# An attention, gate and MLP block in split float32: two W_out blocks moved ahead of the projection, and the MLP's right factors laid out in two pools

## The chip, the cores and the metric

The kernel runs on one core of one Trainium2 chip. The metric is the device time of one execution in microseconds (us); lower is better. Inputs, weights and output are float32 in device memory, 1024 tokens of width 1024.

## The reference

```python
y = jax.nn.sigmoid(gate_a) * (o_a @ w_up_nsa[l]) + jax.nn.sigmoid(gate_b) * (o_b @ w_up_swa[l])
h = h + rms_norm(y @ w_out[l], norm_mix_post[l])
u = rms_norm(h, norm_mlp_pre[l])
f = jnp.square(jax.nn.relu(u @ w_mlp_in[l])) @ w_mlp_out[l]
h = h + rms_norm(f, norm_mlp_post[l])
```

`o_a` (sparse attention with compressed, selected and window keys) and `o_b` (window attention with sinks) are made by the first half of the kernel, which the change leaves as it is. `w_out` is 1024x1024, `w_mlp_in` 1024x4096, `w_mlp_out` 4096x1024.

## The kernel before

Every matrix is kept as two halves: a rounded high part (ACT copies it, `split` L81-91 or `load_w` L108) and the rest, a low part (a subtraction on DVE, L91, or shared between DVE with five eighths and POOL with three eighths, L116). A product is then three matmuls, high with high, high with low and low with high (`mm3`). So a weight block that comes from device memory passes a DMA into `wraw`, ACT (`wh`) and DVE, at times with POOL (`wl`), before TensorE (PE) can use both halves.

The stages that matter here, in order:

- **Gates** (L755-774). Eight rounds over `dc`, 128 columns of the two up-projections each. A round loads the up weights and two gate tiles `gt`, runs four groups of 12 matmuls, multiplies by the sigmoid (DVE L771, L773) and splits the result into `yh[c]`, `yl[c]`, for the two halves `c` of the tokens. The left inputs lie in `oh0`..`oh7`, `ol0`..`ol7`.
- **Output projection** (`out_proj` L822-839), four calls, two blocks of 128 tokens each. A call goes over eight blocks of W_out, 128x1024 (512 KB): load and split by `load_w`, then 12 matmuls L124-126. There are two `wraw` slots in pool `wq`; the first call puts `wh`, `wl` in `wq` too, the others in pool `we`. In the calls on `c` = 0 the low part is shared by DVE and POOL, in those on `c` = 1 DVE makes it alone.
- **Norms and transposes**, then **MLP1** (`prod` L957-959), seven products of a Strassen-like scheme over pairs of 128 columns; its right factors are `bh[i]`, `bl[i]` (and a seventh, `bh7h`, `bh7l`, in tiles tagged u7). Its results are combined (c, q; L1035-1066) and stored to device memory as seven operands `f_d`.
- **MLP2** (`product` L1145-1165), seven products in the order 1, 2, 5, 3, 6, 4, 7, each of 8 steps `kc` and 24 matmuls a step. A step needs `fh`, `fl` (from `fraw`, loaded by L1135 from `f_d`) and `vh`, `vl` (from a tile `b` of w_mlp_out, L1104). Each of the four names has four buffers in pool `st2`; `fraw` has three.

The code is written in the order above and a list scheduler decides the place of each instruction in its engine's queue; pools decide which memory lies over which. `st2` takes the memory that MLP1's right factors leave: `vh` over factor 3, `vl` over 6, `fh` over 4, `fl` over the u7 tiles. So the first writes into `fh` and `fl` have to follow MLP1's last readers of those factors. In `out_proj` the two `wraw` slots lie over `oh2`, `oh3`, which the last group of gate matmuls reads. SP issues most loads, in one queue; ACT issues the two loads of `x` (`hb`, L845); POOL the last five `fraw` and last three `b` of the first MLP2 product.

Of the kernel before, what the change touches and what calls it, by code (L numbers as in the profile page):

```python
# [8 lines left out]
F32 = mybir.dt.float32  # L9
F32R = mybir.dt.float32r  # L10
# [5 lines left out]
P = 128  # L16
# [12 lines left out]
CUT = (5, 5)  # L29
# [5 lines left out]
WEB = 3  # L35
# [10 lines left out]
NG = 4  # L46
# [6 lines left out]
def tile_hybrid_block(ctx: ExitStack, tc: tile.TileContext, x, norm_mix_pre, norm_mix_post, norm_mlp_pre,  # L53
                      norm_mlp_post, w_in, cmp_pos_k, cmp_w1_k, cmp_w2_k, cmp_pos_v, cmp_w1_v, cmp_w2_v,
                      attn_sinks, rel_bias, w_up_nsa, w_up_swa, w_out, w_mlp_in, w_mlp_out, onehot, out):
    nc = tc.nc
    x, out, w_in = x[0], out[0], w_in[0]
    w_up_nsa, w_up_swa, w_out, w_mlp_in, w_mlp_out = (w[0] for w in (w_up_nsa, w_up_swa, w_out, w_mlp_in, w_mlp_out))

    def pool(name, bufs=1, side="left", space=None):  # L60
        kw = {} if space is None else {"space": space}
        if space is not DRAM:
            kw["reuse_waits"] = "tile"
        if space is None:
            kw["side"] = side
        return tc.tile_pool(name=name, bufs=bufs, **kw)
# [17 lines left out]
    def split(h, l, src, h_eng="act", l_eng="dve"):  # L84

        if h_eng == "act":
            nc.scalar.activation(h, src, AF.Copy)  # L87
        else:
            nc.vector.tensor_copy(h, src)
        eng = nc.vector if l_eng == "dve" else nc.gpsimd  # L90
        eng.tensor_tensor(l, src, h.bitcast(F32), op=ALU.subtract)  # L91
# [80 lines left out]
    with ExitStack() as s_u:  # L172
# [8 lines left out]
        kc = pv.tile([P, 2, 2, HD], F32R, name="kc")  # L181
# [27 lines left out]
        with ExitStack() as s:  # L209
# [6 lines left out]
            vh = vt.tile([P, NB, NV], F32R, name="vh")  # L216
            vl = vt.tile([P, NB, NV], F32R, name="vl")
# [25 lines left out]
            with ExitStack() as s0:  # L243
# [28 lines left out]
                for b in range(NB):  # L272
# [11 lines left out]
                    r = rstd_of(tp, ss)  # L284
# [455 lines left out]
    with ExitStack() as s:  # L740
        s_y = s.enter_context(ExitStack())
        yp = [s_y.enter_context(pool("y0", side="right")), s_y.enter_context(pool("y1", side="right"))]
        yh = [p.tile([P, NB, 512], F32R, name="yh", tag="yh") for p in yp]
        yl = [p.tile([P, NB, 512], F32R, name="yl", tag="yl") for p in yp]
        s_ps = s.enter_context(ExitStack())
        pp = s_ps.enter_context(pool("ps2", space=PSUM))
        ps_any = lambda: pp.tile([P, 512], F32, name="ps", tag="ps", bufs=6)
        with s_ot:
            dp = s_ot.enter_context(pool("dtmp"))
            for dc in range(8):  # L750
                cs = slice(dc * P, (dc + 1) * P)
                wh, wl = load_w([((slice(None), slice(0, 4), slice(None)),
                                  w_up_nsa[:, cs].rearrange("(k p) c -> p k c", p=P)),
                                 ((slice(None), slice(4, 8), slice(None)),
                                  w_up_swa[:, cs].rearrange("(k p) c -> p k c", p=P))], [8, P])  # L755
                sig = []
                for b in range(2):
                    gt = dp.tile([P, T], F32, name="gt", tag="gt", bufs=4)
                    nc.sync.dma_start(gt, gate_d[b * D + dc * P:b * D + (dc + 1) * P, :])
                    nc.scalar.activation(gt, gt, AF.Sigmoid)  # L760
                    sig.append(gt)
                for c in range(2):
                    ts = slice(c * 512, (c + 1) * 512)
                    t = []
                    for b in (1, 0):
                        ps = ps_any()
                        for k in range(4):
                            kk = b * 4 + k
                            mm3(ps, wh[:, kk, :], wl[:, kk, :], oh_[kk][:, ts], ol_[kk][:, ts], k == 0, k == 3)
                        tt = dp.tile([P, 512], F32, name="tt", tag="tt", bufs=4)  # L770
                        nc.vector.tensor_tensor(tt, ps, sig[b][:, ts], op=ALU.mult)  # L771
                        t.append(tt)
                    nc.vector.tensor_tensor(t[0], t[0], t[1], op=ALU.add)  # L773
                    split(yh[c][:, dc, :], yl[c][:, dc, :], t[0])
        s_w.close()


# [8 lines left out]
        wp2 = s_w2.enter_context(pool("wq"))  # L786
# [14 lines left out]
        eh = s_e.enter_context(pool("etmph"))  # L801
        hb_e.update({b: eh.tile([P, D], F32, name="hb", tag="hb", bufs=2) for b in (0, 1)})
        s_we = s_e.enter_context(ExitStack())
        we = s_we.enter_context(pool("we"))
        wor = w_out.rearrange("(k p) c -> p k c", p=P)
        ssp = [ep.tile([P, 2], F32, name="ssp", tag="ssp", bufs=8) for _ in range(NB)]

        hbs = {}
        started = []

        def out_proj(c, ts_, nhs, xs_=(), at=0):
            pss = {(t, nh): ps_any() for t in ts_ for nh in nhs}
            n = 1024 // (512 * len(nhs))
            for k2 in range(NB // n):
                wh, wl = load_w([(None, wor[:, n * k2:n * k2 + n, 512 * nhs[0]:512 * nhs[-1] + 512])],
                                [n, 512 * len(nhs)], *((wp2, 2) if not started else (we, WEB)), cut=CUT[c], rpool=wp2, l_eng="dve" if c else None)
                if k2 == at:
                    with tc.issue_after(last_act[0].ins):
                        for b in xs_:
                            load_x(b, nc.scalar)  # L820
                for j in range(n):
                    k = n * k2 + j  # L822
                    for t in ts_:
                        ts = slice(t * P, (t + 1) * P)
                        for i, nh in enumerate(nhs):
                            ns = slice(i * 512, (i + 1) * 512)
                            mm3(pss[t, nh], yh[c][:, k, ts], yl[c][:, k, ts], wh[:, j, ns], wl[:, j, ns],
                                k == 0, k == NB - 1)
            started.append(1)
            for t in ts_:  # L830
                b = c * 4 + t
                if b not in o1:
                    o1[b] = (ea if b % 4 < 2 else ep).tile([P, D], F32, name="o1",
                                                           tag="o1a" if b % 4 < 2 else "o1b", bufs=2)
                for nh in nhs:
                    ns = slice(nh * 512, (nh + 1) * 512)
                    junk = we.tile([P, 512], F32, name="junk", tag="junk", bufs=1)
                    nc.scalar.activation(junk, pss[t, nh], AF.Square, accum_out=ssp[b][:, nh:nh + 1])
                    nc.vector.tensor_tensor(o1[b][:, ns], pss[t, nh], gpost[:, ns], op=ALU.mult)

# [70 lines left out]
        load_x(2)  # L911
        load_x(3)
        out_proj(0, (2, 3), (0, 1), (4, 5), 3)
        norm_t(0)
        norm_t(1)
# [8 lines left out]
        s_we.close()  # L924
        s_y.close()
        s_u2r = s.enter_context(ExitStack())
        u1 = s_u2r.enter_context(pool("u1", side="right"))
        bh, bl = {}, {}
        for i in (5, 3, 6, 4):
            bh[i] = u1.tile([P, 4, 512], F32R, name=f"bh{i}")  # L930
            bl[i] = u1.tile([P, 4, 512], F32R, name=f"bl{i}")

        def u7(name, dt):
            return [u1.tile([P, 4, 512], dt, name=name + t, tag="u7" + t) for t in "hl"]
# [156 lines left out]
        m2a = s.enter_context(pool("m2a"))  # L1091
        m2 = s.enter_context(pool("m2"))
        st2 = s.enter_context(pool("st2", side="right"))
        pq = s.enter_context(pool("ps3", space=PSUM))
        xs = [pq.tile([P, 512], F32, name=f"xs{t}") for t in range(4)]
        ys = [pq.tile([P, 512], F32, name=f"ys{t}") for t in range(4)]
# [40 lines left out]

        def f_op(i, kc):
            raw = f1.pop(kc) if i == 1 and kc in f1 else load_f(i, kc)
            h = st2.tile([P, 2, 512], F32R, name="fh", tag="fh", bufs=NG)  # L1140
            l = st2.tile([P, 2, 512], F32R, name="fl", tag="fl", bufs=NG)
            split(h, l, raw)
            return h, l

        def product(i, bank, first, last):  # L1145

            n = NG if last and i == 7 else 1
            for k0 in [*range(NK - n), NK - n]:
                ks = range(k0, k0 + (n if k0 == NK - n else 1))
                hl = {}  # L1150
                for kc in ks:
                    src = operand(i, kc)
                    vh = st2.tile([P, 2, 512], F32R, name="vh", tag="vh", bufs=NG)
                    vl = st2.tile([P, 2, 512], F32R, name="vl", tag="vl", bufs=NG)
                    hl[kc] = f_op(i, kc) + (vh, vl)
                    split(vh, vl, src)
                for t in range(4):
                    ts = slice(t * P, (t + 1) * P)
                    for kc in ks:
                        fh, fl, vh, vl = hl[kc]  # L1160
                        for j in range(2):
                            a = first and kc == 0 and j == 0
                            z = last and kc == NK - 1 and j == 1
                            for l_, r_, a_, z_ in ((fh, vh, a, False), (fh, vl, False, False), (fl, vh, False, z)):
                                nc.tensor.matmul(bank[t], l_[:, j, ts], r_[:, j, :], start=a_, stop=z_,  # L1165
                                                 skip_group_check=True)
# [105 lines left out]
```

## Time and profile before

| | us |
|---|---|
| three runs | 1576.17, 1577.01, 1580.71 |
| median | 1577.01 |
| profiled execution, its own time | 1580.5 |
| span of its trace | 1578.7 |
| PE busy (share of the span) | 1487.3 (94%) |
| DVE, ACT, POOL busy | 1088.4 (69%), 751.2 (48%), 439.8 (28%) |
| mean granted clock of PE | 0.981 |

A line of a timeline gives start, duration, engine, source line, operation and tiles, and in brackets how long the engine had been idle and what ended that. The clock is a share of full speed: 1.00 is 2.4 GHz, 0.50 is 1.2 GHz. DMA share is the mean busy share of the core's 16 DMA engines.

### The profile page before, as it was taken

The page shows a single profiled execution, that of the slowest core. Times are in us where ns is not written, and L with a number is a line of the kernel's source. Part 1 is how long each engine was busy: PE and PEld are TensorE (multiplying, and loading weights), DVE is VectorE, ACT ScalarE, POOL GpSimd, SP SyncE. Part 2 cuts the span into 40 slices and gives each one's busy share as a digit, 9 for nine tenths or more (in the row PEclk, how much of TensorE's full clock was granted, in tenths as well). Part 3 has the DMA queues.
Part 4 walks back from the last instruction along what each step waited for, and adds up shares of the span by engine and source line. Part 5 has one row for each costly group of instructions (what it writes and reads, how often), then busy time and mean ns, then how long its engine had stood idle before and what let it go on. Part 6 is the DMA issues. An engine that isn't in the chain of part 4 may idle for free. (4 is left out here: it accounts for less than half of the span.)

```text
span 1578.7 us, 20103 instructions
## 1 busy us (share of the span) xinstructions
PE 1487.3 (94%) x6920; PEld 1214.2 (77%) x6920; DVE 1088.4 (69%) x2086; ACT 751.2 (48%) x1461; POOL 439.8 (28%) x354
## 2 busy tenths in 40 slices
PE   6998999999899999999988978999999899999997
PEld 5897888878777777778866766778888688888886
DVE  5455775598964998836537787877757566594775
ACT  5343675576653766653336563332222334334543
POOL 3000351132310232231133014867555410000302
PEclk9999999999999999999999998999999999999999
DMA  7733125111132111164256652444443598263451
GB/s 201 256 103 82 38 51 154 41 44 31 34 97 51 47 34 31 34 225 139 94 186 229 225 159 58 158 162 156 147 153 134 208 336 302 94 188 118 150 184 54
DMA packets 162038, 204.79 MB, mean 130 GB/s; under 512 B 15120, under 2 KB 105264, under 8 KB 161936
## 3 DMA queue, kind: packets, MB, share of 16 engines
q1 hardware_dynamic: 154224, 180.68, 36.5%
q0 software_dynamic: 6992, 20.48, 3.7%
q10 hardware_dynamic: 720, 2.36, 0.4%
q8 instruction: 54, 0.88, 0.2%
q14 instruction: 48, 0.39, 0.1%
HBM read 153.02 MB, written 58.32 MB: 134 GB/s over the span
## 5 line engine op out<-in xcount | busy, mean ns | idle before, releaser
L124 PE MATMUL mm<-uh,wh 128*128 128x512 f32 x464 | 201.4, 434 | 4.1 <-DVE qb L448 3.2
L510 POOL TENSOR_TENSOR e<-e,w 128x256 f32<-128x256 f32 (+7 forms) x128 | 111.6, 898 | 286.4 <-DVE w L648 148.9
L125 PE MATMUL mm<-ul,wh 128*128 128x512 f32 x464 | 184.9, 398 | 0.0
L126 PE MATMUL mm<-uh,wl 128*128 128x512 f32 x464 | 184.5, 398 | 0.0
L87 ACT ACTIVATE th<-pt 128x512 fp32r<-128x512 f32 (+1 forms) x178 | 105.1, 593 | 95.0 <-PE pt L520 84.9
L502 ACT ACTIVATE e<-e,nm 128x256 f32<-128x256 f32 (+7 forms) x192 | 124.4, 649 | 36.8 <-DVE nm L496 36.4
L91 DVE TENSOR_TENSOR tl<-pt,th 128x512 fp32r<-128x512 f32 x162 | 110.0, 682 | 33.8 <-ACT th L87 32.7
L87 ACT ACTIVATE fh<-fraw 128x1024 fp32r<-128x1024 f32 x56 | 59.4, 1062 | 145.3 <-PE xs L1165 78.3
L87 ACT ACTIVATE wh<-wraw 128x1024 fp32r<-128x1024 f32 x69 | 73.0, 1058 | 111.1 <-PE mm L125 36.7
L91 DVE TENSOR_TENSOR fl<-fraw,fh 128x1024 fp32r<-128x1024 f32 x56 | 69.2, 1241 | 78.2 <-ACT fh L87 78.2
L520 PE MATMUL pt<-ident,e 128*128 128x128 f32 x648 | 104.8, 276 | 1.9 <-DVE e L513 0.9
L1165 PE MATMUL xs<-vl,fh 128*128 128x512 f32 x256 | 100.7, 393 | 4.2 <-DVE vl L91 4.2
L126 PEld LDWEIGHTS mm<-uh,wl 128*128 128x128 f32 x464 | 88.0, 190 | 20.9
L124 PEld LDWEIGHTS mm<-uh,wh 128*128 128x128 f32 x464 | 88.9, 192 | 17.4 <-issue 3.3
L91 DVE TENSOR_TENSOR wl<-wraw,wh 128x1024 fp32r<-128x1024 f32 x53 | 69.0, 1301 | 45.9 <-ACT wh L87 45.5
L1165 PE MATMUL xs<-vh,fl 128*128 128x512 f32 x256 | 100.5, 393 | 0.0
L1165 PE MATMUL xs<-vh,fh 128*128 128x512 f32 x256 | 100.2, 392 | 0.0
L1188 POOL TENSOR_TENSOR cc<-cc,gB 128x512 f32<-128x512 f32 x14 | 24.3, 1759 | 269.0 <-ACT sq L1187 267.3
L520 PEld LDWEIGHTS pt<-ident,e 128*128 128x128 f32 x648 | 81.7, 141 | 22.7 <-issue 2.5
L125 PEld LDWEIGHTS mm<-ul,wh 128*128 128x128 f32 x464 | 89.0, 192 | 12.0
L116 POOL TENSOR_TENSOR wl<-wraw,wh 128x384 fp32r<-128x384 f32 (+2 forms) x26 | 38.7, 1493 | 161.7 <-ACT wh L108 161.7
L91 POOL TENSOR_TENSOR wl<-wraw,wh 128x1024 fp32r<-128x1024 f32 x16 | 38.6, 2410 | 159.5 <-ACT wh L87 159.5
(286 smaller groups left out, 4086.0 us busy)
## 6 DMA issues: line engine op xcount, KB each, us to landing
fraw<-f_d SPq DMA_DIRECT2D x48, 512.0 KB, 3.6
wraw<-in_w_mlp_in_dram SPq DMA_DIRECT2D x36, 512.0 KB, 4.5
wraw<-in_w_out_dram SPq DMA_DIRECT2D x32, 512.0 KB, 3.6
f_d<-q SPq DMA_DIRECT2D x64, 256.0 KB, 3.6
b<-in_w_mlp_out_dram SPq DMA_DIRECT2D x32, 512.0 KB, 10.8
wraw<-in_w_in_dram SPq DMA_DIRECT2D x27, 512.0 KB, 4.7
f_d<-c SPq DMA_DIRECT2D x48, 256.0 KB, 4.0
gate_d<-gst SPq DMA_DIRECT2D x32, 256.0 KB, 2.1
```

The source lines that it names most:

```text
L87: nc.scalar.activation(h, src, AF.Copy)
L91: eng.tensor_tensor(l, src, h.bitcast(F32), op=ALU.subtract)
L116: eng.tensor_tensor(lv[:, a:b], rv[:, a:b], hv[:, a:b].bitcast(F32), op=ALU.subtract)
L124: nc.tensor.matmul(ps, ah, bh, start=first, stop=False)
L125: nc.tensor.matmul(ps, ah, bl, start=False, stop=False)
L126: nc.tensor.matmul(ps, al, bh, start=False, stop=last)
L502: nc.scalar.activation(e[:, :n], e[:, :n], AF.Exp, scale=-1.0, bias=nm[:, r:r + 1], accum_out=sm[:, r:r + 1])
L510: nc.gpsimd.tensor_tensor(res[r][:, :n], res[r][:, :n], w[:, r:r + 1].to_broadcast([P, n]), op=ALU.mult)
L520: tr = nc.tensor.transpose(pt[:rows, r, :], es[r][:, off:off + rows], ident)
L1165: nc.tensor.matmul(bank[t], l_[:, j, ts], r_[:, j, :], start=a_, stop=z_, skip_group_check=True)
L1188: (nc.vector if b == NB - 1 else nc.gpsimd).tensor_tensor(cc[:, ns], cc[:, ns], gB[:, ns], op=ALU.mult)
```

## The change

Three parts. First, a pool `wo` takes the first two W_out blocks of the first call: both loads stand in the code of the gates' sixth round, block 0 is split there (ACT, then DVE alone), block 1 at the head of `out_proj` into the `wh`, `wl` of `wq`. The pool `we` is opened only after the first call. Second, MLP1's right factors 5, 3, 6 go to a pool `u1a` and factor 4 with the u7 tiles to `u1`. Third, the four buffers of `fh`, `fl`, `vh`, `vl` in MLP2 are split: steps with kc%4 = 3 use a pool `st3` with one buffer each, the others `st2` with three each; `st2` now lies over factors 5, 3, 6 alone, `st3` over the seventh. No arithmetic is changed.

```diff
+        wo = s_wo.enter_context(pool("wo", side="right"))
...
+        def wo_load(k):
+            r = wo.tile([P, 1, 1024], F32, name="wraw", tag="wraw", bufs=2)
+            nc.sync.dma_start(r, wor[:, k:k + 1, :])
+            wo_raw.append(r)
...
+                if dc == 5:
+                    wo_load(0)
+                    wo_load(1)
+                    wo_hl += [wo.tile([P, 1, 1024], F32R, name=n, tag=n) for n in ("wh", "wl")]
+                    split(*wo_hl, wo_raw[0])
...
+                if started or k2 > 1:
+                    wh, wl = load_w([(None, wor[:, n * k2:n * k2 + n, 512 * nhs[0]:512 * nhs[-1] + 512])],
...
+                elif k2:
+                    wh, wl = (wp2.tile([P, 1, 1024], F32R, name=n_, tag="w" + n_[1], bufs=2) for n_ in ("wh", "wl"))
+                    split(wh, wl, wo_raw[1])
+                else:
+                    wh, wl = wo_hl
...
+            if not started:
+                s_wo.close()
+                we.append(s_we.enter_context(pool("we")))
...
+        u1a = s_u2r.enter_context(pool("u1a", side="right"))
         u1 = s_u2r.enter_context(pool("u1", side="right"))
...
-            bh[i] = u1.tile([P, 4, 512], F32R, name=f"bh{i}")
-            bl[i] = u1.tile([P, 4, 512], F32R, name=f"bl{i}")
+            bh[i] = (u1 if i == 4 else u1a).tile([P, 4, 512], F32R, name=f"bh{i}")
+            bl[i] = (u1 if i == 4 else u1a).tile([P, 4, 512], F32R, name=f"bl{i}")
...
+        st3 = s.enter_context(pool("st3", side="right"))
+
+        def st_tile(name, kc):
+
+            p, n = (st3, 1) if kc % NG == NG - 1 else (st2, NG - 1)
+            return p.tile([P, 2, 512], F32R, name=name, tag=name, bufs=n)
...
-            h = st2.tile([P, 2, 512], F32R, name="fh", tag="fh", bufs=NG)
-            l = st2.tile([P, 2, 512], F32R, name="fl", tag="fl", bufs=NG)
+            h, l = st_tile("fh", kc), st_tile("fl", kc)
...
-                    vh = st2.tile([P, 2, 512], F32R, name="vh", tag="vh", bufs=NG)
-                    vl = st2.tile([P, 2, 512], F32R, name="vl", tag="vl", bufs=NG)
+                    vh, vl = st_tile("vh", kc), st_tile("vl", kc)
```

The order of instructions at three places. ACT, from the gates' last splits (`yh`) into the first W_out blocks (`wh`); before:

```order
L760 ACTIVATE gt<-gt 128x1024
L87 ACTIVATE yh<-tt 128x512 x4
L108 ACTIVATE wh<-wraw 128x1024 x5
L845 DMA hb<-in_x_dram 128x1024 x2
L108 ACTIVATE wh<-wraw 128x1024 x4
```

and now:

```order
L771 ACTIVATE gt<-gt 128x1024
L87 ACTIVATE yh<-tt 128x512 x3
L87 ACTIVATE wh<-wraw 128x1024
L87 ACTIVATE yh<-tt 128x512
L108 ACTIVATE wh<-wraw 128x1024 x3
L869 DMA hb<-in_x_dram 128x1024 x2
L108 ACTIVATE wh<-wraw 128x1024 x4
```

Block 1's high part stands ahead of the last `yh`, and block 0's (not in the rows) some 30 instructions earlier, in the gates' third round; its load stands in SP's queue behind the up weights of that round, with block 1's, ahead of the round's two `gt` loads. PE's queue keeps its order.

DVE, from MLP1's last combinations into MLP2's first splits (`fl`, `vl`); before:

```order
L1046 TENSOR_TENSOR c<-ps,c 128x512
L1058 SCALAR_TENSOR_TENSOR c<-c 128x512
L1054 TENSOR_TENSOR c<-ps,p_11545 128x512
L1058 SCALAR_TENSOR_TENSOR c<-c 128x512
L1063 TENSOR_TENSOR q<-c_11525,c 128x512
L91 TENSOR_TENSOR fl<-fraw,fh 128x1024
L91 TENSOR_TENSOR vl<-b_11670,vh 128x1024
L91 TENSOR_TENSOR fl<-fraw,fh 128x1024
```

and now:

```order
L1072 TENSOR_TENSOR c<-ps,c 128x512
L1084 SCALAR_TENSOR_TENSOR c<-c 128x512
L91 TENSOR_TENSOR fl<-fraw,fh 128x1024
L91 TENSOR_TENSOR vl<-b_11679,vh 128x1024
L91 TENSOR_TENSOR fl<-fraw,fh 128x1024
L1080 TENSOR_TENSOR c<-ps,p_11550 128x512
L91 TENSOR_TENSOR vl<-b_11683,vh 128x1024
L91 TENSOR_TENSOR fl<-fraw,fh 128x1024
```

The first two `fl` and the first `vl` moved ahead of the combination that reads MLP1's last matmul result (L1054 before, L1080 now).

SP, the first loads of MLP2's second product; before:

```order
L1104 DMA b_12152<-in_w_mlp_out_dram 128x2x512
L1104 DMA b_12188<-in_w_mlp_out_dram 128x2x512
L1104 DMA b_12224<-in_w_mlp_out_dram 128x2x512
L1104 DMA b_12264<-in_w_mlp_out_dram 128x2x512
L1135 DMA fraw<-f_d 128x2x512
L1104 DMA b_12301<-in_w_mlp_out_dram 128x2x512
```

and now (the numbers of the same tiles are higher by 9):

```order
L1137 DMA b_12125<-in_w_mlp_out_dram 128x2x512
L1137 DMA b_12161<-in_w_mlp_out_dram 128x2x512
L1168 DMA fraw<-f_d 128x2x512
L1137 DMA b_12197<-in_w_mlp_out_dram 128x2x512
L1137 DMA b_12233<-in_w_mlp_out_dram 128x2x512
L1137 DMA b_12273<-in_w_mlp_out_dram 128x2x512
```

The product's first `fraw` load moved from behind nine `b` loads to behind six; its second and third stay where they were, behind 17 `b` loads and that `fraw`.

## Rows read from the trace of the kernel before

**Rows 1.** Waits of PE, whole span (waiter <- awaited: total us, times, longest)
```profile
PE ps L124 <- ACT wh L108: 8.3, 6, 4.6
PE xs L1165 <- DVE vl L91: 4.2, 1, 4.2
```

**Rows 2.** Timeline of PE, end of the gates and first W_out blocks
```profile
794.75 0.39 PE L126 MATMUL ps<-oh,wl 128*128 128x512 f32 x1
799.74 2.07 PE L124 MATMUL ps<-wh,yh 128*128 128x512 f32 x4 [4.60 <-ACT wh L108]
804.19 1.09 PE L124 MATMUL ps<-wh,yh 128*128 128x512 f32 x4
...
806.99 1.09 PE L124 MATMUL ps<-wh,yh 128*128 128x512 f32 x4
...
820.50 1.20 PE L124 MATMUL ps<-wh,yh 128*128 128x512 f32 x4 [2.08 <-ACT wh L108]
826.73 0.74 PE L124 MATMUL ps<-wh,yh 128*128 128x512 f32 x2 [0.37 <-ACT wh L108]
```

**Rows 3.** Windows (stretch, length, busy PE, PEld, DVE, ACT, POOL, clock, DMA share, GB/s)
```profile
800.00:802.00 2.00, 2.00 (x5) 1.55 (x6) 1.39 (x2) 1.06 (x1) 2.00 (x2) 0.50 0.00 0
820.00:822.00 2.00, 1.50 (x7) 1.23 (x7) 0.82 (x1) 1.44 (x2) 1.48 (x1) 1.00 0.08 31
```

**Rows 4.** Timeline of SP and of ACT, loads and high parts of W_out
```profile
792.22 0.33 SPq L82 DMA_DIRECT2D gpre<-in_norm_mlp_pre_dram  x1
794.49 20.11 SPq L100 DMA_DIRECT2D wraw<-in_w_out_dram  x7
798.63 1.06 ACT L108 ACTIVATE wh<-wraw 128x1024 fp32r<-128x1024 f32 x1 [1.38 <-DMA wraw<-in_w_out_dram]
811.46 1.06 ACT L108 ACTIVATE wh<-wraw 128x1024 fp32r<-128x1024 f32 x1 [2.87 <-DMA wraw<-in_w_out_dram]
819.39 1.06 ACT L108 ACTIVATE wh<-wraw 128x1024 fp32r<-128x1024 f32 x1 [4.52 <-DMA wraw<-in_w_out_dram]
```

**Rows 5.** Timeline of ACT and DVE in the gates' third round
```profile
719.29 1.06 ACT L108 ACTIVATE wh<-wraw 128x1024 fp32r<-128x1024 f32 x1 [7.79 <-PE ps L125]
718.34 1.29 DVE L771 TENSOR_TENSOR tt<-ps,gt 128x512 f32<-128x512 f32 x2 [4.17 <-PE ps L126]
```

**Rows 6.** Windows, norms before MLP1 (columns as in rows 3)
```profile
945.00:950.00 5.00, 1.22 (x2) 0.50 (x2) 4.89 (x4) 3.72 (x8) 4.84 (x4) 0.50 0.01 2
```

**Rows 7.** Timeline of PE and chain that ended last, start of MLP2 (start, us, what)
```profile
1257.74 0.39 PE L1165 MATMUL xs<-vh,fh 128*128 128x512 f32 x1
1262.36 45.91 PE xs L1165 x191
1308.27 43.52 PE ys L1165 x192
```

**Rows 8.** Timeline of DVE, end of MLP1 and start of MLP2
```profile
1254.81 0.69 DVE L1058 SCALAR_TENSOR_TENSOR c<-c 128x512 f32<-128x512 f32 x1
1261.08 1.22 DVE L91 TENSOR_TENSOR vl<-b,vh 128x1024 fp32r<-128x1024 f32 x1
1271.08 0.69 DVE L1066 TENSOR_TENSOR q<-c,q 128x512 f32<-128x512 f32 x1
```

**Rows 9.** Timeline of SP and ACT, loads of MLP2's second product
```profile
1272.70 13.65 SPq L1104 DMA_DIRECT2D b<-in_w_mlp_out_dram  x9
1310.30 1.06 ACT L87 ACTIVATE fh<-fraw 128x1024 fp32r<-128x1024 f32 x1 [0.44 <-DMA fraw<-f_d]
```

**Rows 10.** Windows in MLP2's first product (columns as in rows 3)
```profile
1262.00:1264.00 2.00, 1.64 (x4) 1.35 (x5) 2.00 (x3) 0.00 (x0) 0.45 (x2) 0.50 0.51 123
1300.00:1310.00 10.00, 10.00 (x46) 8.29 (x45) 10.00 (x10) 4.55 (x7) 0.00 (x0) 1.00 1.05 387
```

**Rows 11.** Timeline of POOL, ACT and DVE, steps 5 of MLP2's first product
```profile
1273.92 2.16 POOL L1104 DMA_DIRECT2D b<-in_w_mlp_out_dram  x3
1283.94 1.06 ACT L87 ACTIVATE vh<-b 128x1024 fp32r<-128x1024 f32 x1 [2.00 <-DMA b<-in_w_mlp_out_dram]
1276.54 1.23 DVE L91 TENSOR_TENSOR fl<-fraw,fh 128x1024 fp32r<-128x1024 f32 x1 [2.50 <-ACT fh L87]
```

More of the change, by code (lines that the diff above doesn't have):

```diff
@@ L744, in tile_hybrid_block @@
         yl = [p.tile([P, NB, 512], F32R, name="yl", tag="yl") for p in yp]
+        s_wo = s.enter_context(ExitStack())
+        wo = s_wo.enter_context(pool("wo", side="right"))
+        wor = w_out.rearrange("(k p) c -> p k c", p=P)
+        wo_raw, wo_hl = [], []
+        def wo_load(k):
+            r = wo.tile([P, 1, 1024], F32, name="wraw", tag="wraw", bufs=2)
+            nc.sync.dma_start(r, wor[:, k:k + 1, :])
+            wo_raw.append(r)
         s_ps = s.enter_context(ExitStack())
@@ L803, in tile_hybrid_block @@
         s_we = s_e.enter_context(ExitStack())
-        we = s_we.enter_context(pool("we"))
-        wor = w_out.rearrange("(k p) c -> p k c", p=P)
         ssp = [ep.tile([P, 2], F32, name="ssp", tag="ssp", bufs=8) for _ in range(NB)]
         hbs = {}
-        started = []
+        started, we = [], []
         def out_proj(c, ts_, nhs, xs_=(), at=0):
@@ L814, in out_proj @@
             for k2 in range(NB // n):
-                wh, wl = load_w([(None, wor[:, n * k2:n * k2 + n, 512 * nhs[0]:512 * nhs[-1] + 512])],
-                                [n, 512 * len(nhs)], *((wp2, 2) if not started else (we, WEB)), cut=CUT[c], rpool=wp2, l_eng="dve" if c else None)
+                if started or k2 > 1:
+                    wh, wl = load_w([(None, wor[:, n * k2:n * k2 + n, 512 * nhs[0]:512 * nhs[-1] + 512])],
+                                    [n, 512 * len(nhs)], *((we[0], WEB) if started else (wp2, 2)), cut=CUT[c],
+                                    rpool=wp2, l_eng="dve" if c else None)
+                elif k2:
[3 more added lines that the diff above has]
+                    wh, wl = wo_hl
                 if k2 == at:
@@ L836, in out_proj @@
                     ns = slice(nh * 512, (nh + 1) * 512)
-                    junk = we.tile([P, 512], F32, name="junk", tag="junk", bufs=1)
+                    junk = we[0].tile([P, 512], F32, name="junk", tag="junk", bufs=1)
                     nc.scalar.activation(junk, pss[t, nh], AF.Square, accum_out=ssp[b][:, nh:nh + 1])
```

## The prediction

> **What bounds the kernel now.** I read the waits of PE over the whole span first, since PE is busy 94% of it: the reader is to see that the two waits which the change can reach are those for the first high parts of W_out (8.3 us in six waits, the longest 4.6) and one of 4.2 us for a low part in MLP2 [rows 1]. Then the two places, each in the timelines.
>
> At the output projection PE ends the gates at 794.75 + 0.39 = 795.14 and starts block 0 only at 799.74. Block 0 then takes until 804.19, 4.45 us, where block 1 takes 806.99 - 804.19 = 2.80 [rows 2]: the clock stood at 0.50, 1.2 GHz, in that stretch, after the engine had been idle for 4.60 us. After the idle 2.08 us ahead of 820.50 it stood at 1.00 [rows 3]. From there the stage is bound by its supply: two raw slots, each passing DMA, ACT and the two low-part engines before it is free. The high parts of blocks 0, 4 and 6 start at 798.63, 811.46 and 819.39 [rows 4]: two pairs in 12.83 us, 6.4 a pair, and 7.9 for the pair that shares the queues with the loads of x. PE needs 5.6 for a pair, so it waits at every second block.
>
> At the start of MLP2 one matmul runs at 1257.74, and the other 191 of the first product start at 1262.36 and take 45.91 us, where the second product's 192 take 43.52 [rows 7]. The product lasts 1308.27 - 1257.74 = 50.53, 7.0 more than it needs: 4.2 idle and the rest at the lower clock, 0.50 [rows 10]. What PE waits for is `vl` of step 0, at 1261.08 on DVE [rows 8]; ahead of it in DVE's queue stand the combinations of MLP1's last results.
>
> **The change, part by part.**
>
> *W_out during the gates.* Added there: two loads on SP, one ACT copy (1.06) and one DVE subtraction of 1024 columns, priced 1.22 by the like one at 1261.08 [rows 8]. ACT is idle 7.79 us ahead of 719.29 and DVE 4.17 ahead of 718.34, both for PE [rows 5], and their additions stand just ahead of these rows: cost nothing. POOL loses two low parts. If the cover were gone, 1.2 us of DVE would lie on the gates once. In SP's queue the two issues push the next `gt` loads by about 1 us, inside the same idle stretch: nothing.
>
> *Block 0.* Ready 70 us early, so PE goes on at 795.14 and keeps its clock. That removes 4.60 idle and 4.45 - 2.80 = 1.65 of low clock, 6.25 in all. Block 1 needs its `wh` (ACT, ahead of the last `yh`, after PE's last reads of `oh2`, some 0.7 us before the gates end) and a DVE subtraction: done by about 797, wanted at 797.94. It hides; without that cover each us late is a us of PE.
>
> *Supply one pair ahead.* Blocks 2 and 3 are now the first to use the raw slots, which lie over `oh6` and `oh7`: the last reads of these are in the group before the last, 12 matmuls or 2.8 us sooner. SP could issue block 0's load only at 794.49; now block 2's follows `gpre` at 792.22 with its issue, say 792.7: 1.8 sooner. So block 6 has what block 4 had: high part at 811.46 - 1.8 = 809.7, done 810.7, up to 1.5 (7.9 - 6.4) later for the x loads. PE alone would be there at 795.14 + 6 x 2.80 = 811.94. Block 6 was at 820.50, so 8.2 to 8.6 is won. Block 8 has what block 6 had: 819.39 - 1.8 + 1.06 = 818.7, against 826.73: **8.0**. From here both are bound by supply, so 8.0 is carried. If the slots came no sooner, it would be 6.3. I take 8.0, bounds 6.3 to 8.6.
>
> *Is it kept?* Between the projection and MLP1 DVE is the bound: 4.89 of 5 us busy at 945, PE 1.22 [rows 6]. Its work there needs the projection's results; its queue begins as much sooner. I carry the gain whole and put the other case among the rivals. One low part of factor 5 moves by one place there: at most its own 1.2 us either way, taken as nothing because DVE does the same sum of work.
>
> *MLP2's first splits.* `fh` 0 waits for no MLP1 factor and DVE makes `fl` 0 and `vl` 0 right behind L1058 at 1254.81 [rows 8]: 1254.81 + 0.64 + 2 x 1.14 (1.22 less the overlap of neighbours) = 1257.7, when PE wants them. All 7.0 us could go. But what is late next: step 1 of the second product. PE now wants it at 1257.74 + 43.52 + 5.44 = 1306.70 (a step is 43.52 / 8). Its `fraw` came for the ACT copy at 1310.30 [rows 9]. SP reaches this load behind 17 `b` loads, and these start when L1066, at 1271.08 on DVE, has made the last operand to store. DVE's new order finishes that at about 1269.3 instead of 1271.77: counting from L1058, eight splits at 1.14 and seven short ones at 0.6 to 0.7, with no wait for PE left. That is 2.5 sooner. In between the DMA engines are full (share 1.05 at 387 GB/s from 1300 to 1310 [rows 10]), so what is issued 2.5 sooner lands 2.5 sooner: `fh` at 1307.8, done 1308.9, a wait of 2.2, and `fl` another 0.7: **2.9 lost of 7.0**. A wait of 2.9 lies between 2.08, which kept the clock, and 4.2, which did not, nearer the first; I add half of the 1.65 us that block 0 lost: 0.8. So MLP2 gives 7.0 - 2.9 - 0.8 = **3.3**, bounds 0.7 (the load no sooner, 5.4, and 0.8) and 7.0.
>
> The Trainium skill, "TensorE: Matmul & The Clock Gate", section "HAM oscillation — how this bites in real kernels", says that waits for DMA between bursts of matmuls bring the clock down, so that each next burst starts slow. By that rule the new wait costs its whole low-clock stretch again, 2.6 by estimate from the 45.91 above, and MLP2 gives 1.5. The trace agrees after 4.60 and 4.2 us, not after 2.08.
>
> *Pools of the factors, buffers 3 and 1 in place of 4.* Each step still takes the slot of the step four (kc%4 = 3) or three places before in its own pool; DVE's and ACT's work is the same. Step 5's `vh`, loaded by POOL at 1273.92 and split at 1283.94 [rows 11], is wanted 7.0 sooner and comes some 2.4 sooner: `vl` done at 1283.9, wanted at 1257.74 + 5 x 5.44 = 1284.9. A margin of 1: nothing, up to 2 in the bounds.
>
> **Sum.** 8.0 + 3.3 = 11.3 off the profiled execution's 1580.5, 1569.2. That execution is 3.5 above the median of 1577.01; against the median, **1565.7**.
>
> **The rivals.**
>
> 1. *The full DMA engines give nothing sooner.* SP's earlier `b` loads compete with POOL's last ones and with the stores, and step 1's `fraw` still lands at 1310.3. For it: the share of 1.05, and POOL's loads took 10 us from 1273.92 to 1283.94 [rows 11]. Against: the total to be moved ahead of that load is the same and begins sooner. MLP2 gives 0.7 to 1.5: 9.1 in all, **1567.9**. 0.18.
>
> The Trainium skill, "DMA: Bandwidth & Descriptors", section "Issuing engines are not separate DMA queues", states that transfers issued by several engines run on the same 16 DMA engines and interleave. By that this rival is what saturation looks like; the 10 us of POOL's loads agree.
>
> 2. *All of MLP2's 7.0 is kept*, because the first `fraw`, moved ahead of three `b` loads, and shorter queues bring step 1 in time. It needs 2.9 us more than I count. 15.0 in all, **1562.0**. 0.12.
>
> 3. *The projection's gain is given back* where DVE is the bound [rows 6], if what releases DVE there (a load or an ACT chain) does not move with the projection. For it: PE is mostly idle there, so PE's head start is no help by itself. Against: every input of that stretch comes from the projection. Only 3.3 remains: **1573.7**. 0.08.
>
> 4. *The change does not do what it says.* PE still waits at block 1 or 2, because block 1's split stands in ACT's and DVE's queues among the last gate splits, or SP's load comes no sooner. A wait of 4 us of the 8.0: 7.3 in all, **1569.7**. 0.07.
>
> 5. *Slower: SP stands still.* The second product's first `fraw` now stands behind six `b` loads instead of nine. SP reaches it at about 1270.2 + 6 x 13.65 / 9 = 1279.3 and then waits for a `fraw` buffer, freed by `fl` of step 5 in the first product. Behind it stand 11 `b` loads and the three next `fraw`; on full DMA engines each us of standstill makes step 1 a us later. In the trace that `fl` runs at 1276.54 [rows 11] and it follows PE's pace, which is now faster, so there is no wait. It decides if that `fl` ends after 1279.3 + 11.3 = 1290.6, 13 us later than in the trace; at 1296 the result is 5.4 above the median, **1582.4**. 0.05.
>
> **How the numbers follow.** The forecast has 0.50: between 1563 and 1569. Rivals 1 to 5 have 0.18, 0.12, 0.08, 0.07, 0.05. About 0.3%, 4.7 us, is what a measurement of this kernel can tell from no change, so faster is below 1572.3: the forecast and rivals 1, 2 and 4, 0.87. Same: rival 3, 0.08. Slower: 0.05. The range takes in rivals 2 and 3 and the spread of the runs, 1559.5 to 1575.
>
> **What would show it.** In the new profile: no wait of PE at block 0 and clock 1.00 there; block 8 some 8 us earlier against the gates' end; MLP2's first product in 43.5 to 44; one wait of 2 to 4 us for `fh` or `fl` at the second product's step 1. It is wrong if a wait over 2 us stands at blocks 1 to 3, if the stretch to MLP1's first product is no shorter, or if SP is idle ahead of its first `fraw` load there.

## Result, and the profile after

The changed kernel runs in 1565.74 us (median of four, 1562.88 to 1568.03) against 1576.85 before (four, 1576.17 to 1580.71): ratio 0.9924, 95% interval 0.9901 to 0.9947. Measured once more, six executions beside eleven of the kernel before, it gave 0.9943 (0.9925 to 0.9961). So it is faster by 9 (second measure) to 12 us (first); 11.3 was forecast.

The waits of PE over the whole span of the changed kernel, where [rows 1] stood before:

```profile
PE ps L124 <- ACT wh L108: 4.5, 6, 1.8
PE ys L1196 <- ACT fh L87: 2.6, 1, 2.6
```

The 4.6 us wait at the first W_out block and the 4.2 us wait at MLP2's start are gone. What is left at W_out is short, and one wait of 2.6 us has appeared in MLP2's second product.

The projection first; PE's timeline, answering to [rows 2]:

```profile
793.84 0.40 PE L126 MATMUL ps<-oh,wl 128*128 128x512 f32 x1
794.08 0.39 PE L124 MATMUL ps<-wh,yh 128*128 128x512 f32 x1
...
806.31 1.20 PE L124 MATMUL ps<-wh,yh 128*128 128x512 f32 x4 [0.52 <-ACT wh L108]
...
814.00 1.19 PE L124 MATMUL ps<-wh,yh 128*128 128x512 f32 x4 [1.82 <-ACT wh L108]
...
820.65 0.73 PE L124 MATMUL ps<-wh,yh 128*128 128x512 f32 x2 [0.80 <-ACT wh L108]
```

Block 0 follows the gates' last matmul without a gap, blocks 4, 6 and 8 wait a little. The loads and ACT's high parts, answering to [rows 4], here from block 2 on:

```profile
791.31 0.33 SPq L82 DMA_DIRECT2D gpre<-in_norm_mlp_pre_dram  x1
791.75 40.89 SPq L100 DMA_DIRECT2D wraw<-in_w_out_dram  x12
798.79 1.06 ACT L108 ACTIVATE wh<-wraw 128x1024 fp32r<-128x1024 f32 x1 [2.43 <-DMA wraw<-in_w_out_dram]
805.20 1.06 ACT L108 ACTIVATE wh<-wraw 128x1024 fp32r<-128x1024 f32 x1 [4.06 <-DMA wraw<-in_w_out_dram]
812.89 1.06 ACT L108 ACTIVATE wh<-wraw 128x1024 fp32r<-128x1024 f32 x1 [4.13 <-DMA wraw<-in_w_out_dram]
819.54 1.06 ACT L108 ACTIVATE wh<-wraw 128x1024 fp32r<-128x1024 f32 x1 [3.50 <-DMA wraw<-in_w_out_dram]
```

These are blocks 2, 4, 6, 8. Against the gates' end (793.84 + 0.40 = 794.24, before 795.14) block 8's copy comes 819.54 - 794.24 = 25.30 us behind, block 6's before 819.39 - 795.14 = 24.25 [rows 4]: the supply is one pair ahead, less 1.05. Block 2's load was issued at 791.75 and its copy started 7.04 us later; block 0's before took 798.63 - 794.49 = 4.14.

MLP2: PE's timeline, then the chain that ended last (start, us, what), both answering to [rows 7], then the timeline of DVE and ACT, answering to [rows 8, 9]:

```profile
1246.91 0.39 PE L1196 MATMUL xs<-vh,fh 128*128 128x512 f32 x1
1247.14 0.40 PE L1196 MATMUL xs<-vl,fh 128*128 128x512 f32 x1
```

```profile
1298.67 38.37 PE ys L1196 x168
1337.05 43.52 PE xs L1196 x192
```

```profile
1245.74 1.22 DVE L91 TENSOR_TENSOR vl<-b,vh 128x1024 fp32r<-128x1024 f32 x1
1257.54 0.69 DVE L1092 TENSOR_TENSOR q<-c,q 128x512 f32<-128x512 f32 x1
1297.57 1.06 ACT L87 ACTIVATE fh<-fraw 128x1024 fp32r<-128x1024 f32 x1 [5.34 <-DMA fraw<-f_d]
```

The first `vl` is made while MLP1 still runs, and the second matmul follows the first. The first two products end at 1337.05, 1337.05 - 1246.91 = 90.14 after the start; before it was 1308.27 + 43.52 - 1257.74 = 94.05 [rows 7]. So MLP2 gave 3.9. The chain between (start, us, what) shows what the new wait hangs on:

```profile
1257.54 0.70 DVE q L1092
1258.26 0.32 SPq L1094
...
1260.78 15.09 DMA b<-in_w_mlp_out_dram
1275.88 10.82 DMA b<-in_w_mlp_out_dram
1286.78 10.77 DMA fraw<-f_d
1297.57 1.07 ACT fh L87
1298.67 1.43 PE ys L1196 x5
```

MLP1's last operand, its store, then 26 us of `b` tiles, then the operand that PE waits for.

The profiled executions differ by 1580.5 - 1565.77 = 14.7, more than the medians. Lined up matmul by matmul: 0.9 lies ahead of the gates' end (795.14 against 794.24) and stands already at 600 us, where the programs do the same; 5.2 at the projection, up to block 8 (826.73 - 820.65 - 0.9); 3.9 in MLP2. Of the 4.7 that remain nearly all lies at three places between, where PE's clock was low before and not after. The windows there, before, then after (columns as in [rows 3]):

```profile
902.00:904.00 2.00, 2.00 (x9) 1.62 (x8) 2.00 (x2) 0.97 (x1) 0.00 (x0) 0.54 0.24 96
964.00:966.00 2.00, 2.00 (x7) 1.54 (x6) 1.52 (x3) 0.00 (x0) 0.00 (x0) 0.50 0.66 187
1032.00:1034.00 2.00, 2.00 (x6) 1.57 (x5) 1.52 (x3) 0.00 (x0) 0.00 (x0) 0.50 0.07 27
```

```profile
895.00:897.00 2.00, 2.00 (x14) 1.73 (x14) 2.00 (x2) 0.86 (x1) 0.00 (x0) 1.00 0.51 193
955.00:957.00 2.00, 1.59 (x8) 1.33 (x8) 2.00 (x4) 0.00 (x0) 0.00 (x0) 1.00 0.11 28
1022.00:1024.00 2.00, 1.83 (x8) 1.51 (x9) 1.97 (x4) 0.00 (x0) 0.00 (x0) 1.00 0.34 126
```

Whether that is the change's doing or chance is a question for the experiments.

### The profile page after: what moved, and what is told of

It reads as the page before. It is cut to its first block, busy times and chain, and to the rows that moved or that the text cites. A ratio compares the mean times of both kernels' runs of the same rounds, so it can differ in the third digit from the quotient of the medians.

```text
span 1564.0 us, 20090 instructions
## 1 busy us (share of the span) xinstructions
PE 1479.5 (95%) x6920; PEld 1207.1 (77%) x6920; DVE 1087.0 (70%) x2086; ACT 751.1 (48%) x1461; POOL 435.0 (28%) x352
## 5 line engine op out<-in xcount | busy, mean ns | idle before, releaser
L91 DVE TENSOR_TENSOR wl<-wraw,wh 128x1024 fp32r<-128x1024 f32 x55 | 72.5, 1319 | 50.8 <-ACT wh L87 50.3
L87 ACT ACTIVATE ws_h<-wraw 128x512 fp32r<-128x512 f32 x48 | 30.1, 629 | 106.2 <-PE ps L984 100.6
```

## Experiments

**Each part alone.** The first kernel has the W_out part, the second the pools:

```diff
-            bh[i] = (u1 if i == 4 else u1a).tile([P, 4, 512], F32R, name=f"bh{i}")
-            bl[i] = (u1 if i == 4 else u1a).tile([P, 4, 512], F32R, name=f"bl{i}")
+            bh[i] = u1.tile([P, 4, 512], F32R, name=f"bh{i}")
+            bl[i] = u1.tile([P, 4, 512], F32R, name=f"bl{i}")
...
-            p, n = (st3, 1) if kc % NG == NG - 1 else (st2, NG - 1)
+            p, n = st2, NG
```

> Only the first part of the change: two W_out blocks loaded during the gates; the MLP's pools as before. Theory from the two traces (each part is worth what its own place shows): block 8 of the projection some 6 us earlier than before, MLP2's first product still 50 us with its 4.2 us wait for vl; about 6 us below before, so 1571 against 1577, plus whatever low-clock stretches between 890 and 1040 us happen to be missing. As my prediction's sum had it: 8.0 us, 1569. Rival (the gain is given back where DVE is the bound, ahead of MLP1): under 2 us, 1575 or more.

> Only the second and third part: MLP1's right factors in two pools and MLP2's split buffers 3 and 1; the W_out loads as before. Theory: MLP2's first product takes 43.5 us without its wait, and one wait of 2 to 3 us stands at step 1 of the second product, so 3 to 4 us below before, 1573. Rival (full DMA engines give nothing sooner): 1.5 us or less, 1575.5. Rival that the two parts need each other: no gain, 1577. Up to 900 us its program is that of before, so a low-clock stretch at 902 us should come back if it belongs to the program; if it is missing here, such stretches come and go between executions.

Twelve executions of the first, eleven of the second, beside 22 of before (median 1576.24): 0.9967 (0.9955 to 0.9980), that is 5.2 us, and 0.9975 (0.9961 to 0.9989), 3.9 us. The parts add to 9.1 us, inside both intervals of the whole. Their waits of PE from the projection on, the first kernel's:

```profile
PE ps L124 <- ACT wh L108: 5.4, 6, 2.8
...
PE xs L1194 <- DVE vl L91: 4.2, 1, 4.2
```

and the second's:

```profile
PE ps L124 <- ACT wh L108: 9.0, 5, 4.2
...
PE ys L1170 <- ACT fh L87: 2.8, 1, 2.8
```

Each part takes away its own long wait (4.6 us at block 0, 4.2 for `vl`), and the second alone brings the new one. The rivals fall: the projection's gain is not given back ahead of MLP1 (under 2 us lies outside 3.2 to 7.1), and neither part needs the other. One expectation failed: in the first kernel's profile block 8 stands 823.94 - 795.85 = 28.09 us behind the gates' end, only 3.5 less than before (826.73 - 795.14 = 31.59) and not 6. PE waited the 2.8 us ahead of block 6, and the clock was low behind it (0.56 from 817 to 819). At its end this profile is 1580.5 - 1574.29 = 6.2 us shorter all the same, so one place in one profile does not give the part's worth to a microsecond or two.

The second kernel's program up to 900 us is that of before, but the low clock at 902 us did not come back: PE's wait there was 1.0 us, in before 1.9. There was one near 820 us, where before had none. So the missing stretch at 902 is no work of the change. Those at 964 and 1032 stand in later profiles of kernels that carry the whole change (below: 0.58 from 958 to 960 with the POOL edit, 0.50 from 1023 to 1025 with the third block).

**The loads of the norm vectors.**

```diff
-        load_bcast(gpost, norm_mix_post)
...
-        load_bcast(gpre, norm_mlp_pre)
...
+                if not started and k2 == 3:
+                    load_bcast(gpost, norm_mix_post)
+                    load_bcast(gpre, norm_mlp_pre)
```

> The changed kernel, with the loads of the two norm vectors gpost and gpre (broadcast to 128 rows) issued behind W_out blocks 2 and 3 instead of ahead of them. In the changed kernel block 2's load is issued at 791.75 and its high part starts at 798.79, 7 us later, with the DMA share at 1.00 and 0.88 meanwhile. Theory: the vectors' transfers hold it up; here it lands within 4 to 5 us, blocks 2 and 3 some 2.5 us sooner, and the waits at blocks 4, 6 and 8 (0.5, 1.8, 0.8) go: 1.5 to 3 us below the changed kernel, about 1563. Rival: the W_out loads slow each other and the supply chain keeps its pace: no change, within 0.5 us of the changed kernel.

The timeline of SP and ACT in this kernel, blocks 2 and 3:

```profile
789.05 1.01 SPq L100 DMA_DIRECT2D wraw<-in_w_out_dram  x2
790.11 0.42 SPq L82 DMA_DIRECT2D gpost<-in_norm_mix_post_dram  x1
...
794.45 1.04 ACT L108 ACTIVATE wh<-wraw 128x1024 fp32r<-128x1024 f32 x1
```

Block 2 landed 3.5 us after its issue, where the changed kernel's took 7.0, and was copied right behind the last `yh` (793.91 + 0.63): the vectors did hold it up. PE's waits for these high parts fall from 4.5 to 1.6 us in the stretch, as the theory said. PE's start of block 8:

```profile
816.32 0.74 PE L124 MATMUL ps<-wh,yh 128*128 128x512 f32 x2 [0.21 <-ACT wh L108]
```

The gates end at 792.42 here, so block 8 stands 23.90 behind them, 7.7 less than before: with the vectors out of the way the projection is worth at block 8 what I had forecast, 8.0. The time did not follow: 1567.55, ratio 0.9944 (0.9927 to 0.9961), the same as the changed kernel's second measure. Some 2 us at this place are inside the interval, and this run doesn't show that they reach the end.

**The second product's operands through POOL.**

```diff
-            eng = nc.gpsimd if i == 1 else nc.sync
+            eng = nc.gpsimd if i == 1 or (i == 2 and kc < 3) else nc.sync
```

> The changed kernel, with the first three fraw loads of MLP2's second product issued by POOL, whose queue is empty there, instead of SP, where they stand behind the b loads. Theory: the 2.6 us wait at the second product's step 1 is one of place in the queue, not of the DMA engines' rate; it goes, and SP no longer stands 3 us at the product's first fraw: 2 to 3 us below the changed kernel. Rival (the DMA engines are full, so what comes sooner there makes a b tile as much later): the wait moves to another step and the time is within 0.7 us.

1567.89, ratio 0.9951 (0.9934 to 0.9969): no gain. The high parts of steps 1 and 2 are now in time: ACT copies both from 1296.77 on, and PE begins step 1 at 1300.56. But the wait is not gone, it moved to the low part of step 1. PE, SP and DVE:

```profile
1306.48 0.79 PE L1196 MATMUL ys<-vh,fl 128*128 128x512 f32 x1 [3.95 <-DVE fl L91]
```

```profile
1264.04 29.04 SPq L1137 DMA_DIRECT2D b<-in_w_mlp_out_dram  x17
1294.07 0.37 SPq L1168 DMA_DIRECT2D fraw<-f_d  x1
```

```profile
1294.99 4.62 DVE L1142 TENSOR_TENSOR b<-b,b 128x1024 f32<-128x1024 f32 x4
1300.67 3.49 DVE L1142 TENSOR_TENSOR b<-b,b 128x1024 f32<-128x1024 f32 x3
1305.21 2.35 DVE L91 TENSOR_TENSOR fl<-fraw,fh 128x1024 fp32r<-128x1024 f32 x2
```

PE waits 3.95 us for that `fl`, and the clock stood at 0.50 behind it. DVE is busy without a gap from 1292.71 on, and ahead of the `fl` in its queue stand eight subtractions of `b` tiles for the third product (L1142) and three `vl`. It begins them 1295.12 - 1292.71 = 2.4 us ahead of the second product's start, right behind the landing of a `b` tile at 1292.63; in the changed kernel 1290.47 - 1285.44 = 5.0 ahead. With all 17 `b` loads still in front and POOL's loads beside them, the tiles came later, as the rival had it, and DVE's queue passed that on to the operand. In the changed kernel too DVE was on this work up to 1298.02, 0.6 us before PE went on, so a load in time could not have taken the whole wait away there.

**A third W_out block ahead.**

```diff
+                    wo_load(2)
...
-                if started or k2 > 1:
+                if started or k2 > 2:
...
-                    split(wh, wl, wo_raw[1])
+                    split(wh, wl, wo_raw[k2])
```

> The changed kernel, with a third W_out block loaded during the gates, into the raw slot that block 0's split has left, and split at the gates' end. Theory (the projection is bound by its supply, a pair of raw slots at a time): one block more ahead is worth half a pair, up to 3 us, limited by the 3.1 us of waits that are left at blocks 4, 6 and 8: 2 to 3 us below the changed kernel. Rival: PE's waits there are made up for later, where DVE is the bound, so nothing remains at MLP1's start: within 0.5 us.

1564.19, ratio 0.9922 (0.9908 to 0.9937). PE's waits for high parts from 780 to 920 us are 2.4 us in place of 4.5. Against the changed kernel, 0.9924 and 0.9943, that is 0 to 3 us, not told from none.

**The three together.**

> The three edits together: vectors behind the blocks, three blocks ahead, fraw loads by POOL. Theory: waits in the projection are taken once, not twice (3 us), those of MLP2 beside them (2.6 us): 4 to 6 us below the changed kernel, about 1560. Rival (given back at the DVE-bound stretch and on the full DMA engines): within 1 us of the changed kernel.

1569.49, ratio 0.9954 (0.9937 to 0.9970): no better than the changed kernel, and the theory's 4 to 6 us are excluded. The POOL edit is in it, and its wait (3.4 us, for `fl`) too.

**The changed kernel again, the b loads in the order of need, and that with the third block.** The edit of the second kernel; the third adds that of the third block:

```diff
-            eng.dma_start(raw, f_d[i - 1][2 * kc:2 * kc + 2].rearrange("q p t -> p q t"))
+            f_ins[i, kc] = eng.dma_start(raw, f_d[i - 1][2 * kc:2 * kc + 2].rearrange("q p t -> p q t"))
...
-                load_b(0, 1, kc)
+                with tc.issue_after(f_ins[2, min(kc + 2, 7)].ins):
+                    load_b(0, 1, kc)
```

> The changed kernel itself, to measure it beside the next two on one chip and to see a second profile of it. Theory (the two parts add: 5.2 and 3.9 us): 9 us below before, ratio 0.994. If the first measure, 0.9924, was near its middle: 12 us. The second profile: PE's waits in the projection and at the second MLP2 product the same within 0.3 us; the low-clock stretches that the first profile of it lacked between 890 and 1040 us back in part, since they came and went between the other kernels' profiles over the same code.

> The changed kernel, with each of the b loads for MLP2's third product (the one numbered 5) issued behind a fraw load of the second, two steps ahead of its own number, instead of ahead of all but the first. Theory: the 2.6 us wait comes from 4.5 MB of b tiles that are wanted 40 us later and stand ahead of the second product's operands; it goes and no other step waits: 2 to 3 us below the changed kernel. Rival: SP now stands at fraw loads whose buffers are not free, and the b loads of the second product behind them come late: a wait of 2 us or more at a later step, no gain.

> The edit before this one and the third W_out block together. Theory: 1 to 3 us for the block, 2 to 3 for the loads: 3 to 6 us below the changed kernel, ratio to before 0.991 or less. Rival: within 1 us of the better of the two.

Beside eleven executions of before (1575.94): the changed kernel 1566.55, 0.9943; the order of need 1562.72, 0.9922 (0.9905 to 0.9938); with the third block 1561.49, 0.9918 (0.9902 to 0.9935). The chain of the second:

```profile
1243.96 43.55 PE xs L1199 x192
1287.51 43.52 PE ys L1199 x192
1331.03 43.52 PE xs L1199 x192
```

and SP's loads there:

```profile
1267.12 3.44 SPq L1137 DMA_DIRECT2D b<-in_w_mlp_out_dram  x2
1271.54 2.15 SPq L1171 DMA_DIRECT2D fraw<-f_d  x2
1274.19 0.77 SPq L1137 DMA_DIRECT2D b<-in_w_mlp_out_dram  x1
```

No wait is left in the first two products; step 1's operand is issued at 1271.54, where the changed kernel had 1286.78. The edit also changes DVE's queue: step 1's `fl` starts at 1283.42, ahead of the first subtraction for the third product (1285.08). So the wait was one of order, of the loads and of DVE's work behind them, not of the rate of the DMA engines: all of MLP2's 7.0 us is there to be had. By ratio this kernel is 3.3 us faster than the changed one on the same chip (2 to 3 expected), but the two intervals overlap, so it is the trace that shows the gain, not the time. The third block adds 0.6 us in the ratios (1 to 3 expected), which is nothing that these runs can tell.

The second profile of the changed kernel did not repeat the first as I had expected: PE's waits for W_out's high parts are 3.4 us in place of 4.5, that at step 1 is 1.8 in place of 2.6. The shorter wait at step 1 was followed by low clock, the longer was not. At the three places further up the clock stood at full again, where I had expected low stretches back in part; one stood elsewhere instead (0.50 from 835 to 837), where the first profile has 1.00. Over all eleven profiles one place can be compared exactly: PE's wait for L1046 of before, in MLP1, is 2.39 or 2.4 us in each. The kernel with the W_out part alone, PE's timeline and window:

```profile
1025.79 0.80 PE L982 MATMUL ps<-bh7h,ws_h 128*128 128x512 f32 x1 [2.39 <-DVE c L1071]
```

```profile
1026.00:1028.00 2.00, 2.00 (x5) 1.60 (x6) 1.66 (x3) 0.00 (x0) 0.00 (x0) 0.50 0.15 54
```

and the changed kernel's second profile:

```profile
1018.97 0.50 PE L983 MATMUL ps<-bh7h,ws_h 128*128 128x512 f32 x1 [2.39 <-DVE c L1072]
```

```profile
1019.00:1021.00 2.00, 2.00 (x9) 1.64 (x10) 1.84 (x3) 0.00 (x0) 0.00 (x0) 1.00 0.24 90
```

The same wait, and the clock at half in the one and full in the other. It fell in five of the eleven (before, W_out alone, norm vectors, third block, third block with order of need), so it is not a matter of whether a kernel has the change.

## Why the prediction was right, and which step was not

The time was 1565.74 against 1565.7 forecast, but the terms were 8.0 and 3.3, and the parts alone gave 5.2 and 3.9. The sum of those, 9.1, and the second measure, 9.0, say that the forecast was some 2 us too good, and that the first measure's 11 to 12 us hides it. That the two medians agree to 0.04 us is luck.

- *W_out during the gates costs nothing.* Right: no wait of PE was added up to the gates' end (the 0.9 us between the profiles is the same at 600 us and there), and the third block showed that there is room for one more.
- *Block 0.* Right: no idle time, clock 1.00 there, and (804.19 - 795.14) - (796.82 - 794.24) = 6.5 us won up to block 1, 6.25 forecast.
- *Supply one pair ahead, "1.8 sooner".* This step failed. SP did issue 1.8 sooner: 2.49 us ahead of the gates' end (794.24 - 791.75) against 0.65 (795.14 - 794.49). But the copy of that block began 4.55 us behind the gates' end, against 3.49: the load took 7.04 us in place of 4.14, since the loads of the two norm vectors, issued just ahead of it, were still under way. Putting them behind it brought the copy to within 2.0 us of the gates' end (794.45, where the last gate matmul starts at 792.03 and takes 0.39). I had counted their issue time and not their transfer. So the supply came 1.05 us later against the gates' end and not 1.8 sooner, 2.9 in all, and block 8's gain against the gates' end is 31.59 - 26.41 = 5.2, not 8.0. That is under the 6.3 that I had as the low bound, since I had allowed for a load no sooner but not for one later. Five profiles have the vectors right ahead of this load (the changed kernel's two, W_out alone, POOL, order of need): issue to copy is 6.0 to 7.2 us in them, and block 8's gain 3.5 to 6.8. With the vectors behind it was 7.7. Timed alone the part is worth 5.2 (3.2 to 7.1).
- *Is it kept?* Yes, as far as the time tells: 5.2 (3.2 to 7.1) at the end, and 3.5 to 6.8 at block 8. The extra 2.5 us that block 8 gains with the vectors behind were not found in the time.
- *MLP2, 7.0 less 2.9 less 0.8.* Right in mechanism and size: the last operand was ready 1257.54 - 1246.91 = 10.6 us after the product's start against 13.3, 2.7 sooner (2.5 forecast); the wait at step 1 was 2.6 (2.2 and 0.7); the gain 3.9 in the profile and 3.9 timed. The 0.8 for the clock stood for a loss that came once and once not. It rested on the length of the wait, between 2.08 and 4.2; the trace of before already spoke against that, with low clock behind waits of 1.90 (901.66) and 2.39 us (1031.65). What I overlooked is DVE's queue, which had step 1's `fl` behind the third product's subtractions, 0.6 us short of being the bound itself.
- *Rival 1*, nothing sooner on full DMA engines: wrong for the change itself (the wait is 2.6 us, and MLP2 gave 3.9, not 0.7 to 1.5), and the order of need shows that the rate was not the limit. From MLP1's last operand to the copy of step 1's operand it is 40.0 us (1297.57 - 1257.54), before 39.2: the whole queue moved along, as I had argued. *Rival 2*, all 7.0 kept, did not come by itself, but the order of need gave it. *Rival 3* did not come. *Rival 4* came in part: SP's load was issued sooner and landed no sooner, which took 2.9 us of the 8.0 where I had put 4.

*Rival 5* did not come either, though SP did stand at that load:

```profile
1266.94 3.24 SPq L1168 DMA_DIRECT2D fraw<-f_d  x1
```

It did not stand there for the buffer, since the `fl` of the first product's step 5 was under way at 1260.42. In before the sixth and seventh `b` loads took as long to issue (3.23 us at 1276.74, 3.63 at 1280.02). From the first `b` load to the end of the 17th it is 1285.73 - 1259.37 = 26.4 us, before 25.8, so at most 0.6 us was lost there.

## What to carry to other kernels

When a load is moved ahead, count the transfers that stand just before it in the queue, not only their issues: two small vectors broadcast to 128 rows made a weight block's load 2 to 3 us longer (6.0 to 7.2 us against 4.1). Where a stage starts sooner, look at what the load queue brings first; tiles that are wanted 40 us later can stand ahead of the operand that is wanted next, in the load queue and in the queue of the engine that works on them. Here putting them in the order of need took that wait away, and giving the operand another load queue did not. A single pair of profiles can differ by several us through the clock alone, so take the worth of a part from its own place and from timed runs, not from the ends of two traces.

## What the runs showed that I had not expected

The length of a short wait does not tell the clock behind it: after the same 2.39 us of idle PE it was 0.50 in five profiles and 1.00 in six, and what decided between them these runs do not show. In the kernel before, the twelve matmuls from the one behind that wait take 1035.86 - 1031.65 = 4.2 us from first to last start, in the changed kernel 1024.84 - 1022.17 = 2.7, so one such stretch costs 1.5 us. Three of them make nearly all of the 4.7 us by which the first pair of profiles overstated the change, and several such places in one kernel would explain part of why executions of one program spread over some 8 us (1572.99 to 1581.25 for the kernel before). That was not tried by itself; in 44 recorded executions of the kernel before, time and mean granted clock go together with a correlation of -0.60 (each against the mean of its batch), about a third of the spread.

The Trainium skill, "TensorE: Matmul & The Clock Gate", section "HAM oscillation — how this bites in real kernels", tells of a kernel in which waits for DMA of some 3 to 5 us bring every next burst of matmuls to the low clock. These runs agree for the waits of 4.2 and 4.6 us. In the prediction I let this reach a wait of 2.9 us, which that case does not cover; after 2.4 us here it was low in five cases of eleven.
